# Projection weights split once, kept in DRAM and loaded by the second half of a decoder step

## The chip, the core and the metric

The kernel runs on one core of a Trainium2 chip. A core has TensorE (PE, matmuls into PSUM), VectorE (DVE), ScalarE (ACT) and GpSimd (POOL), which compute on SBUF, and SyncE (SP), which here only issues DMA transfers. Each engine runs its own instructions in the order in which they stand and waits on semaphores for the others. The metric is the device time of one execution in microseconds.

## What is computed

One step of a two-layer decoder in float32, for 1024 prompt tokens and 64 sampled tokens: a layer of stick-breaking attention (16 heads of 64, with a paged cache for the sampled tokens), a layer of RWKV-7 time mixing, and after each a squared-ReLU MLP of 4096 hidden units. Each sub-layer begins with an RMS norm that is modulated by a conditioning vector. The change concerns the projections of the attention layer:

```python
def sb_qkv(h, w_qkv):
    B, T, _ = h.shape
    qkv = (h @ w_qkv).reshape(B, T, 3, SB_HEADS, SB_HEAD_DIM)
    return qkv[:, :, 0], qkv[:, :, 1], qkv[:, :, 2]
...
for i in range(DEPTH):
    hp, gp = ada_norm(xp, c_prompt, norm_mix[i], ada_w_mix[i], ada_b_mix[i])
    ...
    op, kp, vp = sb_mixer_prompt(hp, sb_w_qkv[j], sb_w_o[j], sb_bias[j])
    ...
    xp = xp + gp * sqrelu_mlp(hp, w_up[i], w_down[i])
```

`w_qkv` is 1024 x 3072: 12.6 MB, in 24 tiles of 1024 x 128.

## The kernel before

The 1088 tokens are worked on in two halves, `HALF`: A with 576 columns in two chunks of 288, and B with 512 columns in one chunk. Activations lie with features on partitions and tokens in columns. Each sub-layer runs for A and then for B, with the weights loaded again for B. In the order of the program the foreground has 512 weight tiles: the 24 of q, k, v for A, the 24 of q, k, v for B, then `sb_w_o` and the first MLP for A, the inputs of the time mixing for A, the same for B, and last `rw_w_o` and the second MLP for A and for B.

A product in float32 is made of three matmuls in the faster float32r format. Each operand is split into a rounded part and what is left. For activations these are `hhi` and `hlo` (in the MLP's second matmul `uh` and `ul`), for weights `wh` and `wl`. `weight` loads a tile of 512 KB (`wst`, three buffers) by SyncE, ScalarE rounds it to `wh` by a cast (L342), and GpSimd (L344) and VectorE (L345) each subtract one half to make `wl`. `wh` and `wl` have `WHL` = 3 buffers each. `dense` then does three matmuls for each of the eight k tiles and each chunk (L358 to L360): 48 for a weight in A, 24 of nearly twice the width in B, all into `dq`.

After each foreground group, `step` moves work of the background on. While A's q, k, v are multiplied this is `second`: the RMS norm of B, which reads the eight tiles of x through `Passing` (L102), squares them on ScalarE (`sq`, L265), sums them on TensorE (`ssq`, L267), and spreads the root over the partitions (`rb` from `rv`, L281). While B's are multiplied it is attention for A (transposes `tq`, L140, among it) and the conditioning matmuls with loads `adaw` (L242). Later it is the attention of the sampled tokens, and then the RWKV layer: state units (`rw_units`, with `bkq` at L1174 among the last matmuls of a unit), lanes that invert small triangular blocks on VectorE (`rw_lanes`, L1210 and L1212, stored to `s_tt` and `s_xn` at L1217 and L1220), and chains over the states (`rw_chain`, which loads `st`, `tt`, `Lq`, `x` and `hv` at L1256 to L1268 and begins with `invq` at L1279 and `qc`).

The order on each engine isn't written by hand: the program is recorded and a scheduler, which simulates the time of every instruction, sets the order of the whole program (`schedule_with_timeline_sim=True`). DMA transfers of a queue share eight semaphores, so an issue also waits for the landing of the eighth before it.

Of the kernel before, what the change touches and what calls it, by code (L numbers as in the profile page):

```python
# [10 lines left out]
F32 = mybir.dt.float32  # L11
F32R = mybir.dt.float32r
# [8 lines left out]
NT = 8  # L21
# [12 lines left out]
WHL = 3  # L34
# [72 lines left out]
class Kern:  # L107
# [222 lines left out]
            yield  # L330


    def weight(self, ap):

        nc = self.nc
        kt = ap.shape[1]
        st = self.wp.tile([128, kt, 128], F32, tag="wst", name="wst")
        q = nc.scalar if self.sampling else nc.sync
        q.dma_start(st, ap)
        wh = self.wp.tile([128, kt, 128], F32R, tag="wh", name="wh", bufs=WHL)  # L340
        wl = self.wp.tile([128, kt, 128], F32R, tag="wl", name="wl", bufs=WHL)
        nc.scalar.copy(wh, st)  # L342
        h = kt // 2
        nc.gpsimd.tensor_sub(wl[:, :h], st[:, :h], wh[:, :h].bitcast(F32))  # L344
        nc.vector.tensor_sub(wl[:, h:], st[:, h:], wh[:, h:].bitcast(F32))  # L345
        return wh, wl

    def dense(self, w, mts, hi, lo, pt, ps, evac):

        nc = self.nc  # L350
        kt = len(hi)
        for m in mts:
            wh, wl = self.weight(w[m])
            for c0, n in pt.ch:
                q = ps.tile([128, 512], F32, tag="dps", name="dq")[:, :n]
                for k in range(kt):
                    h, l = hi[k][:, c0:c0 + n], lo[k][:, c0:c0 + n]
                    nc.tensor.matmul(q, wh[:, k, :], h, start=k == 0, stop=False)  # L358
                    nc.tensor.matmul(q, wh[:, k, :], l, start=False, stop=False)  # L359
                    nc.tensor.matmul(q, wl[:, k, :], h, start=False, stop=k == kt - 1)  # L360
                    self.step(n)
                evac(m, c0, n, q)
# [45 lines left out]
    def qkv(self, hi, lo, pt, tmp, ps):  # L408
        I, O = self.I, self.O
        w = I["sb_w_qkv"]  # L410
        out = (O["v_prompt"][0, 0].rearrange("t h d -> t (h d)"),
               O["v_sample"][0].rearrange("b t h d -> (b t) (h d)"))
        self.vp, self.vsd = out
        self.dense_to(w, hi, lo, pt, tmp, ps, self.s_q)
        self.dense_to(w[NT:2 * NT], hi, lo, pt, tmp, ps, self.s_k0)

        def value(m, t):
            self.to_tokens(m, pt, t, *out, tmp, ps)
            self.ready.add(("qkv", pt.o, m))
        self.dense_to(w[2 * NT:], hi, lo, pt, tmp, ps, None, value)  # L420


    def load_tiles(self, src, pt, pool, tag="h"):
# [577 lines left out]
            yield  # L1001
        self.ready.add(("g", pt.o))

    def dense_to(self, w, hi, lo, pt, tmp, ps, dst, then=None, queue=None):

        for m in range(NT):
            t = tmp.tile([128, pt.W], F32, tag="n", name="dn")
            self.dense(w, (m,), hi, lo, pt, ps,
                       lambda m_, c0, n, q, t=t: self.copy(t[:, c0:c0 + n], q))
            if dst is not None:  # L1010
                (queue or self.nc.sync).dma_start(dst[m][:, pt.cols], t)
            if then:
                then(m, t)
# [552 lines left out]
    def rest(self, ctx, lp, hp, xp, tmp, PS):  # L1566
# [44 lines left out]

        x, o = self.next
        dense(I["sb_w_o"], o, A, self.residual(0, x, A, tmp))
        self.show("x1", x, A)
        R = rms(x, A)
# [10 lines left out]
        self.beside(iter(()), 0.0)  # L1626
        x, o = self.next
        dense(I["sb_w_o"], o, B, self.residual(0, x, B, tmp))
        RB = rms(x, B)
        self.ffn(1, x, *norm(1, x, RB, B), B, hp, tmp, PS)  # L1630
# [7 lines left out]
        self.beside(iter(()), 0.0)  # L1638
        x, y = self.next
        dense(I["rw_w_o"], y, A, self.residual(2, x, A, tmp))  # L1640
        self.show("x3", x, A)
        R = rms(x, A)
# [137 lines left out]
```

## Time and profile before

| | us |
|---|---|
| median of 3 runs (lowest, highest) | 3694.59 (3686.51, 3700.34) |
| the profiled execution | 3691.91 |
| its span in the trace | 3690.2 |
| SyncE's queue moved (q1) | 532.90 MB, 44.8% of 16 engines' span |
| HBM read, written | 523.76 MB, 106.01 MB |
| cast `wh` (L342), 512 of them | 424.5, 834 ns each |
| half of `wl` on GpSimd (L344), 512 | 652.7, 1276 ns each |
| half of `wl` on VectorE (L345), 512 | 358.8, 703 ns each |

The means of the last three rows mix two tile sizes: 1024 rows of weight (q, k, v, o, `w_up` and the mixing inputs) and 512 (`w_down`). The profile's first part gives busy time, share of the span and instructions of each engine; its second cuts the span into 40 slices and gives tenths of busy time. The views of stretches used below do the same for any window and add the granted clock of TensorE, the busy share of the 16 DMA engines and their GB/s. In rows of instructions, out<-in are the program's tile names, and a bracket shows idle time before an instruction and what ended it.

### The profile page before, as it was taken

To read this page: it belongs to the slowest core of one execution; us is meant where nothing else is said; L and a number is where in the kernel's file an instruction comes from. 1 tells how busy PE (TensorE), PEld (TensorE's weight loads), DVE (VectorE), ACT (ScalarE), POOL (GpSimd) and SP (SyncE) were. 2 spreads that over 40 slices of the span, in tenths; PEclk is the share of its full clock that TensorE was granted. 3 is DMA by queue.
4 is the path that set the end of the run, shared out by engine and by line. 5 is a ranking of instruction groups with operands and counts; after the bars stand their busy time and mean duration, and the time that the engine had idled before them with its cause. 6 is when DMAs were issued, how large, how long until landed. Compare 5 with 4: busy or idle time off the path is not lost. (4 is left out here: it accounts for less than half of the span.)

```text
span 3690.2 us, 72202 instructions
## 1 busy us (share of the span) xinstructions
PE 3482.2 (94%) x26360; PEld 2770.2 (75%) x26360; DVE 2306.5 (63%) x4718; ACT 1602.1 (43%) x3342; POOL 1223.3 (33%) x1692
## 2 busy tenths in 40 slices
PE   7999999999999999988799998998899999989998
PEld 5986667778888876766577776666788888867887
DVE  4357678885554446687845557657884666645444
ACT  4255566663333345634334445543433444432332
POOL 2344434342222223223433335323222222343332
PEclk8999999999999999988899998999899999989999
DMA  6466653319977785667254445657345444433332
GB/s 237 147 218 209 208 182 121 96 38 333 350 290 263 276 315 174 206 192 210 79 155 133 122 153 159 192 190 219 117 132 144 140 132 122 125 113 114 95 95 83
DMA packets 433014, 634.54 MB, mean 172 GB/s; under 512 B 144337, under 2 KB 244562, under 8 KB 432658
## 3 DMA queue, kind: packets, MB, share of 16 engines
q1 hardware_dynamic: 369394, 532.90, 44.8%
q10 hardware_dynamic: 63264, 97.02, 7.9%
q8 instruction: 209, 3.42, 0.4%
q14 instruction: 147, 1.20, 0.1%
HBM read 523.76 MB, written 106.01 MB: 171 GB/s over the span
## 5 line engine op out<-in xcount | busy, mean ns | idle before, releaser
L344 POOL TENSOR_TENSOR wl<-wst,wh 128x256 fp32r<-128x256 f32 (+1 forms) x512 | 652.7, 1276 | 1432.1 <-ACT wh L342 1214.9
L342 ACT CAST wh<-wst 128x512 fp32r<-128x512 f32 (+1 forms) x512 | 424.5, 834 | 709.9 <-PE dq L359 570.2
L358 PE MATMUL dq<-hhi,wh 128*128 128x288 f32 (+1 forms) x2112 | 711.5, 337 | 21.1 <-ACT hhi L132 19.1
L359 PE MATMUL dq<-hlo,wh 128*128 128x288 f32 (+1 forms) x2112 | 704.0, 334 | 3.7 <-DVE hlo L324 2.9
L360 PE MATMUL dq<-hhi,wl 128*128 128x288 f32 (+1 forms) x2112 | 703.2, 333 | 0.0
L345 DVE TENSOR_TENSOR wl<-wst,wh 128x256 fp32r<-128x256 f32 (+1 forms) x512 | 358.8, 703 | 258.7 <-ACT wh L342 230.4
L358 PE MATMUL dq<-uh,wh 128*128 128x288 f32 (+1 forms) x1536 | 508.9, 336 | 5.3 <-ACT uh L472 2.2
L359 PE MATMUL dq<-ul,wh 128*128 128x288 f32 (+1 forms) x1536 | 507.2, 331 | 0.0
L360 PE MATMUL dq<-uh,wl 128*128 128x288 f32 (+1 forms) x1536 | 505.4, 332 | 0.0
L358 PEld LDWEIGHTS dq<-hhi,wh 128*128 128x128 f32 x2112 | 400.9, 190 | 71.0 <-ACT hhi L132 19.7
L359 PEld LDWEIGHTS dq<-hlo,wh 128*128 128x128 f32 x2112 | 401.0, 190 | 43.3 <-issue 9.3
L360 PEld LDWEIGHTS dq<-hhi,wl 128*128 128x128 f32 x2112 | 400.5, 190 | 36.2 <-issue 6.9
L373 DVE SCALAR_TENSOR_TENSOR x<-dq,mod,x 128x288 f32<-128x288 f32 (+1 forms) x432 | 245.2, 569 | 258.6 <-PE dq L360 255.5
L358 PEld LDWEIGHTS dq<-uh,wh 128*128 128x128 f32 x1536 | 288.1, 188 | 53.6 <-issue 18.0
L548 DVE TENSOR_TENSOR_SCAN prod<-prod 128x256 f32<-128x256 f32 (+5 forms) x264 | 247.9, 941 | 118.0 <-ACT prod L539 76.8
L360 PEld LDWEIGHTS dq<-uh,wl 128*128 128x128 f32 x1536 | 288.4, 188 | 29.6 <-issue 7.1
L359 PEld LDWEIGHTS dq<-ul,wh 128*128 128x128 f32 x1536 | 288.8, 188 | 27.6 <-issue 5.7
L358 PE MATMUL dq<-xhi,wh 128*128 128x288 f32 (+1 forms) x576 | 203.1, 353 | 4.8 <-ACT dn L132 1.8
L359 PE MATMUL dq<-xlo,wh 128*128 128x288 f32 (+1 forms) x576 | 199.7, 347 | 5.8 <-POOL xlo L304 3.9
L360 PE MATMUL dq<-xhi,wl 128*128 128x288 f32 (+1 forms) x576 | 197.5, 343 | 0.0
L470 DVE TENSOR_TENSOR ut<-ut 128x288 f32<-128x288 f32 (+1 forms) x192 | 154.2, 803 | 53.0 <-ACT ut L469 50.1
L472 ACT CAST uh<-ut 128x288 fp32r<-128x288 f32 (+1 forms) x192 | 94.8, 495 | 181.6 <-DVE ut L470 181.2
(300 smaller groups left out, 6234.7 us busy)
## 6 DMA issues: line engine op xcount, KB each, us to landing
pagek<-cache_kT SPq DMA_DIRECT2D x128, 512.0 KB
pagev<-cache_v SPq DMA_DIRECT2D x128, 512.0 KB
adaw<-ada_w SPq DMA_DIRECT2D x192, 256.0 KB
wst<-w_up SPq DMA_DIRECT2D x96, 512.0 KB
wst<-w_down SPq DMA_DIRECT2D x192, 256.0 KB
st<-s_st SPq DMA_DIRECT2D x40, 672.0 KB
wst<-sb_w_qkv SPq DMA_DIRECT2D x48, 512.0 KB
wst<-w_up ACTq DMA_DIRECT2D x32, 512.0 KB
```

Of the source, the lines that this page charges most:

```text
L342: nc.scalar.copy(wh, st)
L344: nc.gpsimd.tensor_sub(wl[:, :h], st[:, :h], wh[:, :h].bitcast(F32))
L345: nc.vector.tensor_sub(wl[:, h:], st[:, h:], wh[:, h:].bitcast(F32))
L358: nc.tensor.matmul(q, wh[:, k, :], h, start=k == 0, stop=False)
L359: nc.tensor.matmul(q, wh[:, k, :], l, start=False, stop=False)
L360: nc.tensor.matmul(q, wl[:, k, :], h, start=False, stop=k == kt - 1)
L373: nc.vector.scalar_tensor_tensor(xs, q[:, :np_], g, xs, ALU.mult, ALU.add)
L470: nc.vector.tensor_mul(t[:, :n], t[:, :n], t[:, :n])
L472: nc.scalar.copy(a, t[:, :n])
L548: nc.vector.tensor_tensor_scan(r, r, r, 1.0 if carry is None else carry, ALU.mult, ALU.bypass)
```

## The change

In A's pass over q, k and v the parts `wh` and `wl` of each of the 24 weights are stored to a DRAM tile `kept` as well (two DMAs of 512 KB on SyncE's queue). In B's pass the load of `wst`, the cast and the two subtractions are left out, and `wh` and `wl` are loaded from `kept` (two DMAs of 512 KB in place of one). So SyncE issues 48 stores more, and 48 loads in place of 24; ScalarE, GpSimd and VectorE have 24 instructions less each. The matmuls are the same.

```diff
-    def weight(self, ap):
+    def weight(self, ap, kept=None, again=False):
...
         kt = ap.shape[1]
+        if again:
+            parts = [self.wp.tile([128, kt, 128], F32R, tag=t, name=t, bufs=WHL)
+                     for t in ("wh", "wl")]
+            for p, src in zip(parts, kept):
+                nc.sync.dma_start(p.bitcast(F32), src)
+            return parts
         st = self.wp.tile([128, kt, 128], F32, tag="wst", name="wst")
...
         nc.vector.tensor_sub(wl[:, h:], st[:, h:], wh[:, h:].bitcast(F32))
+        if kept is not None:
+            nc.sync.dma_start(kept[0], wh.bitcast(F32))
+            nc.sync.dma_start(kept[1], wl.bitcast(F32))
         return wh, wl
 
-    def dense(self, w, mts, hi, lo, pt, ps, evac):
+    def dense(self, w, mts, hi, lo, pt, ps, evac, kept=None):
...
-            wh, wl = self.weight(w[m])
+            wh, wl = self.weight(w[m], kept and kept[m], kept is not None and pt.o > 0)
...
-        self.dense_to(w, hi, lo, pt, tmp, ps, self.s_q)
-        self.dense_to(w[NT:2 * NT], hi, lo, pt, tmp, ps, self.s_k0)
+        if not pt.o:
+            self.kept = self.dram.tile([3 * NT, 2, 128, NT, 128], F32, name="kept")
+        kept = [[self.kept[m, x] for x in range(2)] for m in range(3 * NT)]
+        self.dense_to(w, hi, lo, pt, tmp, ps, self.s_q, kept=kept)
+        self.dense_to(w[NT:2 * NT], hi, lo, pt, tmp, ps, self.s_k0, kept=kept[NT:])
...
-        self.dense_to(w[2 * NT:], hi, lo, pt, tmp, ps, None, value)
+        self.dense_to(w[2 * NT:], hi, lo, pt, tmp, ps, None, value, kept=kept[2 * NT:])
```

`dense_to` hands `kept` on to `dense`. The lines of the changed kernel stand 7 to 14 further down: L342 is now the load from `kept`, L346 the load of `wst`, L354 and L355 the two stores.

SyncE's order at the beginning, where A's first weights are loaded and `second` reads x, was:

```order
L339 DMA wst<-sb_w_qkv 128x1024 x3
L102 DMA x<-x 128x512
L1011 DMA s_q<-dn 128x576
L102 DMA x<-x 128x512
L339 DMA wst<-sb_w_qkv 128x1024
L508 DMA q<-s_q 128x576
L102 DMA x<-x 128x512 x4
```

Now, from the first store to the third load of x on (six of the eight that follow are the rest of the norm's):

```order
L346 DMA wst<-sb_w_qkv 128x1024
L102 DMA x<-x 128x512
L1025 DMA s_q<-dn 128x576
L354 DMA kept<-wh 128x1024
L355 DMA kept<-wl 128x1024
L346 DMA wst<-sb_w_qkv 128x1024
L102 DMA x<-x 128x512
L354 DMA kept<-wh 128x1024
L522 DMA q<-s_q 128x576
L355 DMA kept<-wl 128x1024
L346 DMA wst<-sb_w_qkv 128x1024
L102 DMA x<-x 128x512 x8
```

The third load of x stood right behind the load of q; now `kept<-wl` of the fifth weight and a load of `wst` stand between.

SyncE's order in the second MLP of A, at the end of B's lanes, where the stores of `s_xn` and `s_tt` end and the loads of the state chains begin, was:

```order
L1220 DMA s_xn<-lxn 8x32x32
L1217 DMA s_tt<-llt 8x32x32 x2
L339 DMA wst<-w_up 128x1024 x2
L1256 DMA st<-s_st_9722 128x7x192
L1259 DMA tt<-s_tt 128x192
L1261 DMA Lq<-s_l 128x192
L1266 DMA x_30792<-s_xn 32x96
```

And now:

```order
L1234 DMA s_xn<-lxn 8x32x32
L1231 DMA s_tt<-llt 8x32x32 x2
L346 DMA wst<-w_down 128x512 x2
L1270 DMA st<-s_st_9699 128x7x192
L1273 DMA tt<-s_tt 128x192
L1275 DMA Lq<-s_l 128x192
L1280 DMA x_30769<-s_xn 32x96
```

The two weights loaded between the stores and the chains' loads were tiles of `w_up` (48 matmuls each) and are tiles of `w_down` (24 each). From `st` on 41 loads followed until the next weight, and 53 do now.

TensorE's order where B's first chain begins, `invq`, among the foreground's `dq`, was:

```order
L360 MATMUL dq<-hhi,wl 128x288
L358 MATMUL dq<-hhi,wh 128x288
L1279 MATMUL invq<-x_30792,Lq 32x32 x6
L1319 MATMUL qc<-hv,st 64x64 x2
L359 MATMUL dq<-hlo,wh 128x288
```

And now:

```order
L371 MATMUL dq<-uh,wl 128x288
L369 MATMUL dq<-uh,wh 128x288
L1293 MATMUL invq<-x_30769,Lq 32x32 x6
L1333 MATMUL qc<-hv,st 64x64 x2
L370 MATMUL dq<-ul,wh 128x288
```

`invq` stood in a weight of `w_up` behind 9877 foreground matmuls of the whole program, and stands in one of `w_down` behind 9775; of these 486 lay between the last `bkq` and the first `invq`, and 444 do now.

More of the change, by code (lines that the diff above doesn't have):

```diff
@@ L1002, in rw_gate, with dense_to @@
         self.ready.add(("g", pt.o))
-    def dense_to(self, w, hi, lo, pt, tmp, ps, dst, then=None, queue=None):
+    def dense_to(self, w, hi, lo, pt, tmp, ps, dst, then=None, queue=None, kept=None):
         for m in range(NT):
@@ L1008, in dense_to @@
             self.dense(w, (m,), hi, lo, pt, ps,
-                       lambda m_, c0, n, q, t=t: self.copy(t[:, c0:c0 + n], q))
+                       lambda m_, c0, n, q, t=t: self.copy(t[:, c0:c0 + n], q), kept)
             if dst is not None:
```

## The prediction, made before the changed kernel was run

> **What bounds the kernel now.** I read the profiled execution from the outside in: the totals of the engines, the stretches of 100 us, and then the list of waits of TensorE in the stretches that the change touches. Totals first: per engine the busy time, its share of the span and the number of instructions.
>
> ```profile
> span 3690.2 us, 72202 instructions
> PE 3482.2 (94%) x26360; PEld 2770.2 (75%) x26360; DVE 2306.5 (63%) x4718; ACT 1602.1 (43%) x3342; POOL 1223.3 (33%) x1692
> ```
>
> TensorE is busy for 3482.2 of 3690.2 us. The change takes no matmul away, so a gain can only come out of the remaining 208 us, and only from the part of them in which TensorE waits for weights or for what the freed engines do. The stretches (columns: stretch, length, busy us of PE, PEld, DVE, ACT and POOL with instruction counts, granted clock, DMA share, GB/s) say where those 208 us lie:
>
> ```profile
> 0.00:100.00 100.00, 73.96 (x613) 57.83 (x614) 49.41 (x102) 41.34 (x68) 31.44 (x48) 0.90 0.66 230
> 100.00:200.00 100.00, 100.00 (x773) 98.35 (x772) 31.25 (x55) 32.05 (x57) 30.19 (x36) 1.00 0.42 140
> 200.00:300.00 100.00, 98.95 (x747) 74.73 (x746) 63.37 (x103) 53.34 (x106) 44.38 (x76) 1.00 0.71 239
> 300.00:400.00 100.00, 98.82 (x733) 66.39 (x732) 78.54 (x138) 58.30 (x127) 45.92 (x101) 1.00 0.64 213
> 400.00:500.00 100.00, 99.70 (x729) 66.06 (x727) 67.15 (x115) 52.18 (x108) 39.13 (x80) 1.00 0.65 215
> 900.00:1000.00 100.00, 99.95 (x1001) 81.01 (x999) 51.97 (x107) 33.35 (x72) 25.79 (x40) 1.00 0.90 337
> 2500.00:2600.00 100.00, 86.22 (x574) 70.17 (x574) 69.22 (x149) 41.35 (x75) 30.63 (x38) 0.93 0.70 218
> 2600.00:2700.00 100.00, 83.27 (x632) 71.16 (x633) 89.32 (x216) 41.60 (x83) 19.04 (x26) 0.86 0.41 115
> 2700.00:2800.00 100.00, 94.51 (x720) 90.90 (x719) 73.21 (x176) 32.58 (x65) 28.73 (x31) 0.97 0.48 134
> 2800.00:2900.00 100.00, 100.00 (x971) 87.49 (x971) 57.00 (x152) 42.85 (x122) 23.99 (x26) 1.00 0.46 137
> ```
>
> Half A's projection pass runs from 38 to about 230 us, half B's from there to about 550. From 200 to 500 us TensorE is idle for 1.05 + 1.18 + 0.30 = 2.5 us. What it waited for, in total, times and longest (20 to 260 us, then the longest of 260 to 520 us):
>
> ```profile
> PE ssq L267 <- ACT sq L265: 6.3, 4, 3.3
> PE rb L281 <- DVE rv L277: 3.2, 2, 3.1
> ...
> PE tq L140 <- DVE beta L549: 1.2, 1, 1.2
> ```
>
> Neither list, read to its end, has a wait for a cast or for `wl`: the weights of both passes are ready before TensorE wants them.
>
> **The change part by part.** All sums stand against the profiled execution of 3691.9 us (a span of 3690.2 and 1.7 around it); the median of the runs, 3694.6, is 2.7 above.
>
> *What half B saves: 0 (a gain of 0 to 2.5).* Each of its 24 weights loses one of these (out<-in, shapes, count, busy us, mean ns; 260 to 520 us):
>
> ```profile
> L344 POOL TENSOR_TENSOR wl<-wst,wh 128x512 fp32r<-128x512 f32 x17 | 27.2, 1600 | 35.0 <-ACT wh L342 33.3 <-PE dq L360 1.7
> L345 DVE TENSOR_TENSOR wl<-wst,wh 128x512 fp32r<-128x512 f32 x17 | 17.9, 1052 | 0.9 <-ACT wh L342 0.8
> L342 ACT CAST wh<-wst 128x1024 fp32r<-128x1024 f32 x17 | 17.8, 1049 | 12.7 <-PE dq L359 12.6
> ```
>
> That is 24 x 1.60 = 38 us of GpSimd, 24 x 1.05 = 25 us of VectorE and 25 us of ScalarE. All of it lies beside a TensorE that is idle for 2.5 us there, so 2.5 is the most it can bring, and none of those waits is for these three. I take 0.
>
> *Stores in half A's steady pass: 0 (0 to +23).* SyncE gains two issues for each weight; `kept<-wh` and `kept<-wl` wait for the same cast and subtractions that the next `wst` load waits for already, so nothing new is queued behind a wait. What grows is the traffic. How long a weight of A takes is read from 48 matmuls of the same shape that run back to back in a later stage; these are the first and the last (start, length):
>
> ```profile
> 2784.58 0.30 PE L359 MATMUL dq<-hlo,wh 128*128 128x288 f32 x1
> ...
> 2790.81 0.29 PE L358 MATMUL dq<-hhi,wh 128*128 128x288 f32 x1
> ```
>
> That is 6.23 / 47 = 0.133 us from one to the next, and 6.4 us for the 48 of one weight. Two stores of 128 x 1024 x 4 bytes are 1.05 MB in 6.4 us, 165 GB/s. On top of the 140 GB/s of the row at 100:200 this is 305. That row's own ratio, 140 GB/s at a share of 0.42, gives 305 a share of 0.92: under 1. The row at 900:1000 shows 337 GB/s at 0.90 with TensorE busy for 99.95. I take 0. If a stored byte takes 1.5 times as long as one of that mix, the share is 0.42 + 1.5 x 0.50 = 1.17, and 24 weights of 6.4 us get 17% longer, +26; I keep +23 as the end, since the first of them lie beside the idle time below.
>
> Against this speaks a table of the Trainium skill, "DMA: Bandwidth & Descriptors", section Bandwidth, which puts a 1 MB transfer at 341 GB/s and one of 64 KB at 138, and asks for batches of 1 MiB; its fit of 2.0 us plus bytes over 436 GB/s makes 3.2 us of each 512 KB transfer. One at a time, three of them would take 9.6 us of each 6.4, an estimate of +77 us over the pass by that page. The trace does not bear out that they run one at a time: 900:1000 moves 337 GB/s with transfers of 512 and 256 KB.
>
> *The first weights of half A: +3 (0 to +6).* Here the order moves something onto the path. While the first weights are multiplied, the norm of half B reads x in eight loads; TensorE then stands waiting for their squares. TensorE's rows, with the idle time before them in brackets, and SyncE's loads:
>
> ```profile
> 57.69 0.43 PE L267 MATMUL ssq<-sq,ones 128*32 128x128 f32 x8
> 65.77 0.66 PE L267 MATMUL ssq<-sq,ones 128*32 128x128 f32 x8 [3.28 <-ACT sq L265]
> 70.58 2.05 PE L281 MATMUL rb<-rv,cst 128*128 128x128 f32 x8 [3.06 <-DVE rv L277]
> ...
> 51.36 6.63 SPq L102 DMA_DIRECT2D x<-x  x4
> 57.54 1.03 ACT L342 CAST wh<-wst 128x1024 fp32r<-128x1024 f32 x1
> 66.19 0.63 ACT L265 ACTIVATE sq<-x 128x512 f32<-128x512 f32 x1 [0.47 <-DMA x<-x]
> ```
>
> In the new order the loads of the third to eighth x stand behind `kept<-wl` of the fifth weight, whose cast waits until TensorE has left the second weight. That cast stands at 57.54 now, behind other ScalarE work; without that it can start once the second weight is done. The 120 matmuls that stand before the wait end at 57.6, and the second weight's last is 24 of them earlier, 3.2 us, so near 54.4. With the cast of 1.03 and the subtraction of 1.6 us after it (GpSimd's row above) the store goes at 57.0, 5.7 us after the 51.36 at which these loads go now. So the last square, now ending at 66.8, comes 0 to 5.7 us later, and TensorE waits as much longer. I take 3, the middle: the six loads then follow one another without the wait for q between their squares, which gives part back, and nothing covers the rest. TensorE's other work before that point is the same 120 matmuls.
>
> *The start of half B and the attention beside it: +1 (0 to +8).* The loads of `wh` and `wl` wait for TensorE leaving the weight three back, and each weight is 24 matmuls of twice the width, so they have two weights' time to land; only the third pair stands behind twelve `adaw` loads (11 of them now take 6.32 us to issue) and lands about when it is wanted. The attention of half A stands some 20 transposes later than now at weights 48 to 60 and level again at 64, in a stretch where DVE and TensorE share the waits. I take 1 for both together; the upper end is 3 for the load and 5 for the 20 transposes (0.28 us each, in the row below, is 5.6).
>
> ```profile
> 227.87 6.32 SPq L242 DMA_DIRECT2D adaw<-ada_w  x11
> ...
> L140 PE MATMUL tq<-cst,beta 128*128 128x128 f32 x40 | 6.3, 279 | 0.0
> ```
>
> *The late stretch: +12 (+5 to +28).* No edit touches it, but the written order is made for the program as a whole, and the freed engines shift the state units of the second RWKV half against the MLP matmuls that hide them. Now the chain there runs as follows (start, length): the last `bkq` of the units, the long lane chain on VectorE, its stores, and the loads back, for which TensorE waits 4.0 us:
>
> ```profile
> 2723.70 0.69 PE bkq L1174 x16
> 2788.77 6.23 DMA x<-s_xn
> ...
> 2795.08 0.83 PE L1279 MATMUL invq<-x,Lq 32*32 32x32 f32 x12 [3.99 <-DMA x<-s_xn]
> ...
> 2785.46 1.00 SPq L339 DMA_DIRECT2D wst<-w_up  x2
> 2786.55 0.56 SPq L1256 DMA_DIRECT2D st<-s_st  x1
> 2814.34 0.36 SPq L339 DMA_DIRECT2D wst<-w_down  x1
> ```
>
> From `bkq` to `invq` are 71.4 us of chain. Counted in the order, TensorE has 9877 foreground matmuls ahead of the first `invq` now and 9775 then: 102 x 0.133 = 13.5 us less work is done when it arrives at the wait, and 444 instead of 486 of them lie between `bkq` and `invq`. If the units also end earlier, by up to the 60 matmuls (8.0 us) that stand less ahead of the last `bkq`, that much comes back: +5.5 to +13.5, middle 9.5. Behind the wait, SyncE issues the burst of loads for the state chains, 41 now in the 27.8 us from 2786.55 to 2814.34, and 53 then before the next weight. Twelve loads more are 12 x 27.8 / 41 = 8.1 us; and the two weights loaded just ahead of it are of `w_down` with 24 matmuls each instead of `w_up` with 48, so cover is 48 x 0.133 = 6.4 us shorter. Together 0 to +14.5; of this I take 2.5, near the lower end, since the row at 2800:2900 shows TensorE busy for 100.00 us through the present burst. 9.5 + 2.5 = 12. It is the nearest thing to a guess in the sum, as the same units stand in a stretch where VectorE is busy for 89 of 100 us and may set the pace alone.
>
> The sum: 3691.9 + 0 + 0 + 3 + 1 + 12 = 3707.9, say **3708 us**.
>
> **The rivals.** *(a) The late stretch pays in full.* The units do not end earlier, so TensorE stands 13.5 us longer before `invq`, and the burst starves it for the 14.5 us as well: 3691.9 + 4 + 28 = 3724. For it speaks VectorE's 89.32 in 2600:2700, a chain that foreground order can't hurry; against it the 100.00 behind the present burst. It decides once the units' end moves by less than about 3 us.
>
> *(b) Half A's pass becomes bound by DMA*, if a stored byte takes more than 1.16 times a byte of that mix (0.42 + 0.50 x 1.16 = 1); at 1.5 times it is 3691.9 + 23 + 4 = 3719, with the late stretch at zero. For it: no row shows a stretch in which most bytes are written. Against it: 337 GB/s at 0.90. It is the case to which the page's table points.
>
> *(c) All of it is hidden:* the late order costs as much as the earlier units give back, 3692 within 8.
>
> *(d) Faster.* VectorE and ScalarE, freed early, let the units run ahead by enough to shorten the stretch from 2500 to 2800, where TensorE idles for 13.8 + 16.7 + 5.5 = 36 us. Half of it gone is -18 or so: 3674. Against it: until 2500 us nothing in the order of the units has lost a predecessor, and their chain has the same instructions. That the loads of `kept` merely replace others and nothing moves is case (c).
>
> **How the numbers follow.** Chances: my forecast, with its own range from 3697 to 3722, 0.42; (a) 0.22; (b) 0.08; (c) 0.18; (d) 0.10. A measurement can tell about 0.5% of 3694.6, or 18.5 us, from no change: 3676 and 3713. Of the forecast's 0.42, 0.32 lie under 3713 and 0.10 above. So faster 0.10; same 0.32 + 0.18 = 0.50; slower 0.10 + 0.22 + 0.08 = 0.40. The range takes in (c) below and (a) and (b) above, with what lies around each: 3684 to 3740; (d) is left out.
>
> **What would show it.** The gaps before `ssq` and `rb` near 60 us should add up to about 3 more than now, and the last square should end near 70. From 100 to 200 us TensorE should be at 100 with a DMA share near 0.9; a share at 1 with TensorE waiting for `wh` or `wl` is (b). From 200 to 500 TensorE should lose what it loses now, with VectorE some 8 us less busy in each 100. The wait of `invq` for `x<-s_xn` should grow from 4.0 to about 13 us; if it is 4 or less the term of 12 is wrong, and with it the forecast, which then falls to 3696. A wait of `dq` for weights behind 2800 is the burst. What would make the prediction wrong altogether is a stretch that no edit touches and whose order I have not followed, above all 530 to 800 and 1300 to 1900 us.

## The result, and the profile after

The changed kernel takes 3740.06 us (median, 3738.64 to 3745.6), the kernel before 3697.47 us in the same comparison: a ratio of 1.0119, 95% interval 1.0103 to 1.0135. It is slower by 43 us, where the forecast was 3708 and the range ended at 3740. The profiled execution of the changed kernel has a span of 3737.5 us, 47.3 above that of before.

The totals of the engines show the change itself and nothing of its cost:

```profile
span 3737.5 us, 72216 instructions
PE 3503.2 (94%) x26360; PEld 2792.2 (75%) x26360; DVE 2290.4 (61%) x4694; ACT 1580.0 (42%) x3318; POOL 1188.7 (32%) x1668
```

VectorE, ScalarE and GpSimd each have 24 instructions less and 16 to 35 us less work. TensorE has the same 26360 matmuls and is 21 us longer at them: in stretches with a lower granted clock the same matmul takes longer, as rows of the late stretch show below.

The stretches of 100 us, in the columns of the prediction:

```profile
100.00:200.00 100.00, 100.00 (x773) 98.35 (x772) 29.85 (x54) 32.05 (x57) 32.04 (x36) 1.00 0.83 293
200.00:300.00 100.00, 98.72 (x738) 76.33 (x738) 53.56 (x94) 43.61 (x93) 29.03 (x70) 1.00 0.87 303
300.00:400.00 100.00, 99.03 (x742) 66.11 (x741) 65.35 (x126) 51.63 (x117) 34.26 (x89) 1.00 0.72 238
400.00:500.00 100.00, 97.13 (x687) 64.39 (x687) 57.99 (x106) 42.51 (x97) 27.45 (x71) 0.98 0.77 258
2600.00:2700.00 100.00, 78.82 (x603) 67.49 (x601) 84.73 (x205) 39.55 (x70) 24.72 (x29) 0.85 0.44 122
2800.00:2900.00 100.00, 88.26 (x832) 71.08 (x831) 50.91 (x135) 37.83 (x114) 20.53 (x25) 0.83 0.55 157
```

Half A's steady pass (100 to 200) is at 100.00 with 293 GB/s and a share of 0.83: the stores are hidden there. VectorE is busy 9 to 13 us less in each 100 of half B's pass, and TensorE gains nothing by it. The loss is elsewhere, far from the change: 2800:2900 was at 100.00 before and is at 88.26, at a clock of 0.83.

Windows at fixed times mix a shift with a loss. A better measure is at hand, because both kernels have the same 13824 foreground matmuls (`dq`) in the same order: the **lag**, the start of the k-th `dq` after less that before. At the first `dq` of some weights it reads:

| weight | 0 | 3 | 8 to 24 | 80 | 152 | 164 | 272 | 312 | 328 | 416 | 511 |
|---|---|---|---|---|---|---|---|---|---|---|---|
| lag, us | -1.1 | +5.6 | +5.6 | +8.9 | +7.6 | +15.1 | +15.4 | +32.8 | +30.0 | +47.2 | +47.0 |

(Where the background does not stand at the same place in both orders, a lag also shows which of the two has done more of it: at weight 48 it reads -6.3 and at 360 +73.6, and most of either is gone 32 to 56 weights later. At 8, 80, 272, 328 and 416 I read it as time lost, to a few us.) The first weights cost about 7 us, then the lag grows in steps as far as weight 416, 3300 us into the run. From weight 48 on, all that differs is the order.

### The profile page after: what moved, and what is told of

Its sections match the earlier page's. It is cut to its first block, busy times and chain, and to the rows that moved or that the text cites. A ratio compares the mean times of both kernels' runs of the same rounds, so it can differ in the third digit from the quotient of the medians.

```text
span 3737.5 us, 72216 instructions
## 1 busy us (share of the span) xinstructions
PE 3503.2 (94%) x26360; PEld 2792.2 (75%) x26360; DVE 2290.4 (61%) x4694; ACT 1580.0 (42%) x3318; POOL 1188.7 (32%) x1668
## 5 line engine op out<-in xcount | busy, mean ns | idle before, releaser
L351 POOL TENSOR_TENSOR wl<-wst,wh 128x256 fp32r<-128x256 f32 (+1 forms) x488 | 620.9, 1274 | 1405.6 <-ACT wh L349 1187.3
L349 ACT CAST wh<-wst 128x512 fp32r<-128x512 f32 (+1 forms) x488 | 399.8, 824 | 688.0 <-PE dq L370 531.5
L352 DVE TENSOR_TENSOR wl<-wst,wh 128x256 fp32r<-128x256 f32 (+1 forms) x488 | 329.6, 678 | 272.6 <-ACT wh L349 251.2
L371 PEld LDWEIGHTS dq<-hhi,wl 128*128 128x128 f32 x2112 | 401.0, 190 | 41.3 <-issue 10.3
```

## The experiments

Two theories stood against each other. **WORK**: the cost is in the new transfers and their waits. **ORDER**: it is in the order that the scheduler made for the whole program. To part them, the program was scheduled twice: once as one kernel, to learn the order of its instructions on each engine, and then as the other, with order-only edges between neighbours, so that all instructions that both kernels have stand as in the first. Such an edge lies between two instructions of one engine, which run one behind the other anyway, so no wait should be added. No run of the kernel before with its own edges tests this; the nearest is e7 below, at a ratio of 0.9987.

```python
for e, order in order_of(KERNEL_FOR_ORDER).items():      # per engine, as scheduled
    for a, b in zip(order, order[1:]):
        tc.add_manual_dep(common[e][b], common[e][a].name, no_sync, reason="order")
```

### e1: all of the change's work, in the old order

> All the work of the change (48 stores, 48 loads of the kept parts, no casts or subtractions in half B), but every instruction that both kernels have stands on its engine in the order of the kernel before; only the new transfers find their own places. Theory ORDER (the 43 us come from the rewritten order of the whole program): 3690 to 3705 us. Theory WORK (they come from the traffic and the waits of the new transfers): 3735 to 3745 us. If the stores delay the first x loads even in the old order, 3 to 6 us of it stay.

Ratio 1.0029 (1.0016 to 1.0043), 3703.9 us against 3693.7. Of 43 us some 10 are left, more than the 3 to 6 expected of the start. The lag, from weight 0 on, is +10.3 at weight 8 and +6.5 at the end, with -0.3 at 272 and +9.2 at 328 in between, so it comes at the start, and what follows is no steady growth. ORDER holds for the rest.

### e2: none of the change's work, in the new order

> The kernel before, none of the change's work, but from foreground weight 48 on (the end of half B's q, k, v) every instruction stands in the changed kernel's order. ORDER: the lag that the changed kernel gathers behind weight 48, 3735 to 3745 us. WORK: 3690 to 3700 us.

Ratio 1.0111 (1.0091 to 1.0131), 3734.5 us. This kernel stores and loads nothing new, and loses 41 us by its order alone. From weight 0 on, its lag is +2.0 at weight 272, +19.1 at 328, +33.1 at 416. (The 33 and the 41 differ because the first `dq` of its trace came 4.8 us later than before, and its median is 4 us above its profiled execution, that of before 2 us. So the 10 of e1 and the 41 of e2 need not add up to the 43.)

### e3, e4: the border at weight 48

> The changed kernel's work, its own order up to foreground weight 48, the order of before from there on. ORDER: only the start's 5.6 us are left, 3697 to 3706 us, and the lag stays at about 5 us to the end. WORK or a shift that no order mends: 3730 us or more.

Ratio 1.0048 (1.0033 to 1.0064), 3712.0 us, above what was expected: a lag of +6.0 at weight 8, 6 more by weight 80, nothing from there to weight 272, and some 7 more by the end. Two orders that do not fit each other meet at weight 48, but that need not be the cause: the runs that keep the new order (the change, e10, e11) lose 3.3 to 5.3 us from weight 8 to 80 as well.

> The changed kernel's work, the order of before up to foreground weight 48, free from there on. ORDER with chance in it: the late order is made anew, and lands anywhere between 3690 and 3745 us; if the late order follows from the work alone and not from small shifts, it is again the changed kernel's, 3730 to 3740 us. WORK: 3730 to 3740 us as well, so this run tells only if it is far below.

Ratio 1.0069 (1.0049 to 1.0089), 3721.4 us. The late order was made anew, and it is a third one: its last `bkq` and first `invq` stand behind 9380 and 9858 foreground matmuls, against 9391 and 9877 before and 9331 and 9775 in the changed kernel. It loses 6.6 us between weights 328 and 416 where the changed kernel loses 17.2. So the late order is not given by the change's work; it changes with what stands ahead of it.

### e5, e6, e7: the work alone, part by part, in the old order

> Only the 48 stores are added; half B loads, casts and subtracts its weights as before; everything both have stands in the order of before. If the start's loss comes from the stores (they hold the loads of x and q back on SyncE's queue and share the DMA engines with them): lag +7 to +10 us at the fourth weight, kept to the end, 3700 to 3706 us. If it comes from the order: 3690 to 3697.

> Only half B's part: its 24 weights are loaded as two parts and not cast or subtracted, but only the first weight of half A is stored and all 24 load that one (so half B's q, k, v are of the wrong weights), in the order of before. If freed engines in half B are worth nothing: lag 0 to +2 us throughout, 3692 to 3698 us. If they are worth their idle time: -2 to -3 us by weight 48.

> The whole change except for the first six of the 24 weights, which are split in both halves as before; in the order of before. If the stores among the first weights alone cost the start's 6 to 10 us: lag within 1.5 us of zero at weight 8 and 3690 to 3698 us. If the steady pass pays for stores as well: lag growing from weight 8 to 24, above 3700.

The edit of e7 leaves the first six weights out of `kept`:

```diff
-        kept = [[self.kept[m, x] for x in range(2)] for m in range(3 * NT)]
+        kept = [[self.kept[m, x] for x in range(2)] if m >= 6 else None for m in range(3 * NT)]
```

| | ratio (95%) | lag from weight 0 on, at weight 8 / 80 / end |
|---|---|---|
| e5, stores alone | 1.0030 (1.0012 to 1.0047) | +8.1 / +8.1 / +13.6 |
| e6, half B's part alone | 1.0011 (0.9998 to 1.0023) | -0.6 / -2.2 / +4.1 |
| e7, both, from the seventh weight on | 0.9987 (0.9972 to 1.0002) | +0.2 / -3.8 / -1.6 |

The medians are 3707.2, 3699.9 and 3693.2 us; the first two are 1 to 2 us above what was expected. The stores cost, and only those of the first six weights: without them the change costs nothing that can be measured. Half B's part brings no gain that the times show, as forecast. The lags hint at a small one: from weight 8 to 80 the three runs with that part in the old order go 2.9, 1.6 and 4.0 us ahead (e1, e6, e7), and the two without it 0.0 and -0.2 (e5, e8); one execution cannot settle that. The rows of 40 to 60 us, first of the kernel before, then of the changed one, then of e7, say why the first stores hurt:

```profile
40.00:60.00 20.00, 16.68 (x138) 14.95 (x137) 8.90 (x12) 8.54 (x13) 7.09 (x6) 1.00 0.64 214
40.00:60.00 20.00, 17.62 (x122) 17.19 (x121) 7.14 (x9) 4.58 (x6) 5.61 (x4) 0.88 1.03 386
40.00:60.00 20.00, 18.48 (x124) 17.76 (x125) 9.34 (x19) 6.28 (x9) 4.50 (x4) 0.79 0.57 192
```

In the changed kernel the DMA engines are full in this stretch (1.03, 386 GB/s), just when the norm of half B wants its x and the attention its q. SyncE's issues there, two of ScalarE's rows and TensorE's longest wait:

```profile
48.30 0.33 SPq L1025 DMA_DIRECT2D s_q<-dn  x1
52.24 1.00 SPq L102 DMA_DIRECT2D x<-x  x1
54.05 1.05 ACT L349 CAST wh<-wst 128x1024 fp32r<-128x1024 f32 x1 [5.31 <-PE dq L370]
55.13 0.33 SPq L354 DMA_DIRECT2D kept<-wh  x1
55.55 0.38 SPq L522 DMA_DIRECT2D q<-s_q  x1
57.01 0.32 SPq L355 DMA_DIRECT2D kept<-wl  x1
57.96 15.03 SPq L102 DMA_DIRECT2D x<-x  x8
60.28 0.63 ACT L265 ACTIVATE sq<-x 128x512 f32<-128x512 f32 x1 [4.64 <-DMA x<-x]
...
PE ssq L267 <- ACT sq L265: 11.6, 4, 5.9
```

The store of q goes at 48.30 and the load of it 7.3 us later (before: 47.55 and 50.99). Just ahead of the load stands `kept<-wh`, which waits for the cast that ends at 55.10; `kept<-wl` waits for the subtraction, and the group of x loads behind it starts at 57.96 (before: 51.36). So SyncE's order holds both loads back. They also land later. The second x, issued at 52.24, is there for its square at 60.28, 8.0 us on; before, these were the rows, 3.7 us apart:

```profile
47.93 0.43 SPq L102 DMA_DIRECT2D x<-x  x1
51.67 0.63 ACT L265 ACTIVATE sq<-x 128x512 f32<-128x512 f32 x1 [0.76 <-DMA x<-x]
```

From the load of q to its cast it is 6.6 us (55.55 to 62.17) and was 4.6 (50.99 to 55.62). The wait of `ssq` grows from 6.3 to 11.6 us; in e7 (whose lines stand a few further down) it is 5.2:

```profile
PE ssq L268 <- ACT sq L266: 5.2, 4, 3.2
```

### e8: a small edit

> The kernel before with 24 stores of 64 KB (the first eighth of wh) in half A and nothing else, 1.6 MB in all, order free. If the late order follows from any small shift (chance): it moves by more than 0.3% either way, with lag steps behind weight 150. If it needs the freed engines of half B: within 0.2% of before, 3690 to 3702.

Ratio 1.0003 (0.9993 to 1.0014). The order hardly changed: 2 of 20824 matmuls stand elsewhere. So not every edit makes a new order. This run also shows what one profiled execution is good for: its own took 3710 us against a median of 3697, with a lag 10 us higher between weights 272 and 328, in an order as good as the old one. A step of 10 us in that stretch of one trace is not yet a finding.

### e10, e11: the border further back

> The change as it is up to foreground weight 272, the order of before from there on. In the changed kernel's trace the lag is 15 us at weight 272 and 47 at the end. If the 32 us between come from the order of the units, lanes and chains of the second RWKV half: lag stays at 12 to 18 us, 3706 to 3715 us. If the earlier order has spoilt what comes later: 3725 or more.

Ratio 1.0072 (1.0049 to 1.0096), 3726.0 us against 3700.3. Here the late stretch is mended in full, +25.4 us of lag at weight 328 (from weight 0 on) and +27.0 at 416. Some 7 us are lost where the two orders meet, between weights 272 and 280, which is why the whole is above what was expected. By its time alone the run falls to the other case (3725 us or more); the lag speaks against that, since it grows by only 4.4 us from weight 280 to the end.

> The same from foreground weight 320 on, just ahead of the end of the lanes, their stores and the burst of loads for the chains. The changed kernel's lag is 31 us there and 47 at the end. If the burst between the lanes' stores and the next weights costs the last 16 us, as the prediction had it: lag stays at 28 to 34 us, 3720 to 3730 us. If the place of the units ahead of it forces that cost: 3735 to 3745 us.

Ratio 1.0134 (1.0115 to 1.0153), 3745.9 us: no better than the change. But the run does not tell what it was made to tell. The edges hold what the program's text has behind weight 320, and the chains' loads come earlier in the text: the first `invq` stood behind 9757 foreground matmuls, not at its old place. As a test of that border it is void; for what follows it counts as one more run with a late order close to the changed kernel's.

### e12, e13: each part alone, order free

> Only the 48 stores, half B as before, order free. In the order of before the stores alone gave 1.003. If a new late order is made by half B's freed engines and loads only: 3700 to 3710 us, lag 6 to 10 us from the start to the end. If the shift at the start is enough to make a bad late order: 3720 us or more.

> Only half B's part (24 weights loaded as two parts, all from the one stored weight, so half B's q, k, v are of the wrong weights), order free. If half B's part makes the late order that costs: lag near 0 up to weight 40 and 25 to 40 us at the end, 3720 to 3735 us. If the two parts must act together: within 8 us of before, under 3703.

Ratios 1.0064 (1.0047 to 1.0081) and 1.0079 (1.0058 to 1.0101), 3723.6 and 3730.2 us against 3700.3. In the old order the same two gave 1.0030 and 1.0011. So either part is enough to make a new order, which costs 13 and 25 us beyond that. Each order is another one: of the 20824 matmul instructions that the program of e12, that of e13 and that of the change share with the kernel before, 1674, 5087 and 4580 stand elsewhere in relation to the others. Nor is the cost always late. In e12 the lag grows by 14.1 us between weights 272 and 328 and by 7.9 between 328 and 416. In e13 it falls in both (by 9.5 and 7.9), and the stretch 2800:2900 is at 100.00 as before; its lag grows ahead of weight 272, to +51.7, and ends at +33.6; part of the +51.7 is background done earlier, since its last `bkq` stands behind 9074 foreground matmuls and not 9391. Where e13 loses its time was not found. All four orders that were made anew (the change, e4, e12, e13) are 13 to 33 us slower than the old order with the same work; why the old one is the better is not shown.

## The late stretch

The growth of the lag, stretch by stretch, in the traces whose order there is the changed kernel's (or close to it) and in those that have the order of before:

| weights | new order | old order |
|---|---|---|
| 8 to 80 | +3.3, +4.8, +5.3 (change, e10, e11) | -2.9, 0.0, -1.6, -4.0, +0.2 (e1, e5 to e8) |
| 80 to 272 | +6.5, +4.1, +6.3, +4.5 (change, e2, e10, e11) | -7.7, -1.7, +4.4, -1.3, -2.4, +3.2 (e1, e3, e5 to e8) |
| 272 to 328 | +14.6, +17.1, +15.7 (change, e2, e11) | +9.5, +8.3, +1.1, +7.7, +4.9, +10.0 (e1, e3, e5 to e8) |
| 328 to 416 | +17.2, +14.0, +19.4 (change, e2, e11) | -1.9, -0.8, -0.2, +1.1, +0.1, 0.0, +1.6 (e1, e3, e5 to e8, e10) |

Between weights 328 and 416 the lag grows by 14 to 19 us in the new order and by -2 to +2 in the old. This step is settled. The same pieces as in the prediction, the last `bkq` and the first `invq`, after, with foreground matmuls ahead of the first `invq`:

```profile
2743.53 0.72 PE L1188 MATMUL bkq<-cst,BK 64*128 64x64 f32 x16
...
2803.18 0.29 PE L371 MATMUL dq<-uh,wl 128*128 128x288 f32 x1
2809.70 0.61 PE L369 MATMUL dq<-uh,wh 128*128 128x288 f32 x1 [6.22 <-ACT wh L349]
...
2812.74 0.44 PE L371 MATMUL dq<-uh,wl 128*128 128x288 f32 x1
...
2813.16 0.29 PE L370 MATMUL dq<-ul,wh 128*128 128x288 f32 x1
...
2815.49 0.46 PE L1293 MATMUL invq<-x,Lq 32*32 32x32 f32 x12
```

From `bkq` to `invq` are 72.0 us, and 71.4 before: the chain through VectorE's lanes and the stores keeps its own pace, with less foreground beside it too. What changes is how much foreground lies in it, 444 matmuls in place of 486. The missing time shows as a wait, but not where it was forecast: the first `invq` waits no longer, since a foreground weight waits ahead of it, 6.2 us. Its load stands on SyncE behind the lanes' stores:

```profile
2804.58 1.41 SPq L1231 DMA_DIRECT2D s_tt<-llt  x2
2806.11 1.13 SPq L346 DMA_DIRECT2D wst<-w_down  x2
2807.34 0.56 SPq L1270 DMA_DIRECT2D st<-s_st  x1
...
2843.22 7.25 SPq L346 DMA_DIRECT2D wst<-w_up  x4
```

And the next weights follow only at 2843.22, after 53 loads in 35.9 us. TensorE then has little but the chains' small matmuls: from 2820 to 2840 it starts 3 foreground matmuls, where there were 103 before.

How the loss is shared out can be reckoned from this, with foreground that is not yet done counted at the prediction's 0.133 us. At the last `bkq` the changed kernel is 19.8 us later with 60 matmuls less done, 27.8 us behind; at the first `invq` 20.4 us later with 102 less, 34.0 behind; at weight 416 it is 47.2 behind. So some 6 us are lost between `bkq` and `invq` and some 13 behind `invq`, in and after the burst of loads. In e2 it is 5 and 12, in e11 10 and 12. (The sum is above 17 because weight 328, where the table begins, stands between the last `bkq` and the first `invq`.)

Three stretches of 20 us, of the changed kernel and then of the kernel before:

```profile
2800.00:2820.00 20.00, 13.78 (x108) 12.45 (x107) 4.49 (x10) 2.81 (x8) 2.31 (x4) 0.83 0.66 176
2820.00:2840.00 20.00, 17.04 (x213) 12.46 (x212) 8.20 (x30) 8.97 (x35) 0.00 (x0) 0.58 0.49 134
2840.00:2860.00 20.00, 17.44 (x152) 14.37 (x153) 9.83 (x24) 9.59 (x26) 6.03 (x4) 0.74 0.60 185
2800.00:2820.00 20.00, 20.00 (x228) 17.99 (x228) 7.66 (x23) 7.98 (x26) 0.97 (x1) 0.98 0.58 164
2820.00:2840.00 20.00, 20.00 (x191) 17.96 (x191) 11.68 (x31) 9.09 (x27) 5.47 (x6) 1.00 0.41 124
2840.00:2860.00 20.00, 20.00 (x178) 17.43 (x178) 10.67 (x25) 7.32 (x17) 6.08 (x4) 1.00 0.39 129
```

GpSimd's 0.00 in 2820:2840 is the sign that no weight was being split. TensorE's clock is at 0.83, 0.58 and 0.74: the stretch pays once for the gaps and once for slow matmuls. The rows above show the second: behind the wait of 6.22 us a foreground matmul takes 0.44 us, and 0.29 again from 2813 on; the granted clock is 0.50 from 2806.2 to 2813.0 and 1.00 from there to 2823.2. From 2823.3 to 2843.7 it is 0.50 once more, though the longest wait there is 1.22 us. With the order of before from weight 272 on (e10) the wait is back at `invq`, at its old size:

```profile
2826.90 0.86 PE L1296 MATMUL invq<-x,Lq 32*32 32x32 f32 x12 [4.18 <-DMA x<-s_xn]
```

Between weights 272 and 328, in the state units of the second half, the traces of the new order lie at 14.6 to 17.1 us and those of the old one at 1.1 to 10.0, 6.9 in the mean. So the profiled execution of before was a quick one there, and about 9 us belong to the order. Between 80 and 272 the means are +5.4 and -0.9, about 6 apart, but the traces of the two orders overlap, so that step is likely and not settled. Of weights 280 to about 315 the trace shows nearly the same number of matmuls with more idle time and a lower clock, first before and then after:

```profile
2290.00:2690.00 400.00, 358.16 (x2352) 261.65 (x2353) 289.27 (x656) 192.03 (x375) 121.10 (x148) 0.93 0.57 176
2304.00:2719.00 415.00, 363.59 (x2347) 263.72 (x2347) 298.71 (x668) 194.61 (x379) 127.36 (x149) 0.89 0.56 172
```

Which row of the order costs these 9 us was not found: the waits are spread over many instructions.

## Why the prediction was wrong

The direction was right: +16 us were forecast and +43 came. What was held most likely, no change that can be told (0.50), did not come; slower, with 0.40, did. The terms of the sum beside what the runs show, in us:

| term | predicted | measured | from |
|---|---|---|---|
| half B's savings | 0 (-2.5 to 0) | 0 by the times, at most -4 by the lag | e1, e6, e7 |
| stores in the steady pass | 0 (0 to +23) | 0 | lag flat from weight 8 to 24 |
| first weights of half A | +3 (0 to +6) | +4 to +7 in the new order, +8 to +10 in the old | change, e3, e10, e11; e1, e4, e5 |
| start of half B and attention (weights 8 to 80) | +1 (0 to +8) | +3 to +5 | change, e10, e11 |
| weights 80 to 272 | no term | about +6, not settled | new against old order |
| units, weights 272 to 328 | no term | about +9 | new against old order |
| late stretch, weights 328 to 416 | +12 (+5 to +28) | +17 | change, e2, e10, e11 |

With the change's own +6.7 and +3.3 for the two early terms the measured ones add up to 42, and the comparison says 43. Several of them are known to a few us only, so that they meet so closely is partly luck.

**The step that failed** is the one behind "No edit touches it, but the written order is made for the program as a whole": having seen that the order is new everywhere, the prediction charged it at one place, and let the rest stand at zero. Two stretches had no term and cost about 6 and 9 us, together more than half of the 27 that were missing. It even named stretches "whose order I have not followed" as what could make it wrong, and gave them no width. With 4580 of 20824 matmuls moved, each stretch in which TensorE has idle time needed a bound of its own.

**Mis-sized: the first weights.** The path was right, step by step: `kept<-wl` of the fifth weight went at 57.01 (forecast 57.0), the x loads behind it at 57.96, and the last square was done at 72.6 (forecast near 70, before 66.8). Half of the delay was to be made good by x loads that follow one another; none was. The share of the DMA engines was missing, 1.03 in 40:60: q and the second x not only went later but took 2.0 and 4.3 us longer to land. The size, +4 to +7 in four traces of this order, lies at the upper end of the range. The rival of a pass bound by DMA held from 40 to 60 us, and not for the pass.

**Mis-sized: the late stretch.** +17 lies in the range, but for other reasons than were given. Of the 12, 9.5 were to be lost ahead of `invq` and 2.5 in the burst behind it; it was some 6 ahead and 13 behind. The burst of 53 loads and the missing cover were seen, and priced at 14.5 in full; the small part of it was chosen because 2800:2900 had been at 100.00. That row held the cover that the new order takes away, so it said nothing of the burst without it. The prediction's own sign failed too: `invq` was to wait 13 us, and 4 or less was to mean that the term is wrong and the whole 3696. The first `invq` did not wait at all and the stretch was lost all the same, because a foreground weight waited ahead of it.

**Right, with a bound too small: half B.** The freed engines brought nothing that the times show. The bound of 2.5 us, though, was read from 200 to 500 us, and half B's last `dq` runs at 592; 500:600 has another 1.6 us of idle time (busy 98.38), so the bound was 4.1.

**Right:** the steady pass. 305 GB/s and a share of 0.92 were forecast, 293 and 0.83 measured. From the two rows at 100:200, the added 153 GB/s took a share of 0.41, and the 140 of before 0.42, so a stored byte took no longer here than one of the earlier mix. The table that the Trainium skill gives in "DMA: Bandwidth & Descriptors", section Bandwidth, with 1 MiB as the size to aim at, did not decide here: it is of loads issued from GpSimd, and these are loads and stores issued from SyncE. The same holds of the fit that the prediction puts beside it; it stands in another section of that page, "Anatomy of one DMA — SWDGE (gpsimd) path". The three transfers of 512 KB for each weight overlapped (293 GB/s), and TensorE waited for none (busy 100.00).

## What to carry to other kernels

Where a scheduler orders the whole program, an edit has two prices, that of its work and that of the order that comes with it. Here they were about 10 us (e1) and 33 to 41 (e2, by the lag and by the time), and neither was the gain that the freed engines suggested. Hold the old order by order-only edges and time the edit in it: that separates the two, and tells whether to mend the edit or the order. And compare traces by the lag of one fixed sequence of instructions, not by windows: it shows where time is lost, once the background stands at the same place in both, and the lags of several runs over one stretch show what is noise.

## What the runs showed that was not expected

The background keeps its pace and the foreground fills it: 71.4, 72.0 and 72.0 us from `bkq` to `invq` in the kernel before, the changed one and e10 (2754.87 to 2826.90), with 486, 444 and 486 foreground matmuls in between. A small edit, 24 stores of 64 KB, left the order alone, while either half of the change made a new one. And one stretch of one order differs by 10 us from one profiled execution to another, which is as much as several terms of the sum. TensorE's clock, last, stood at 0.50 for 20 us of small matmuls without a wait above 1.22 us.
